# Layer 0's depthwise convolution: 24 scaled taps, summed by accumulating DMAs before and by additions on POOL after

## The chip, the core and the metric

The kernel runs on one core of one Trainium2 chip. The metric is the device time of one execution in microseconds (us). A core has five engines, each with an instruction queue of its own that is worked off in order: PE (TensorE, matmuls), DVE (VectorE), ACT (ScalarE), POOL (GpSimd) and SP (SyncE, which here only issues DMAs). On-chip data lies in SBUF as 128 partitions by some number of columns; matmul results lie in PSUM. Engines wait for one another through semaphores.

## The reference

The model is a two-layer diffusion backbone over 256 context tokens and 1024 latent tokens of width 1024. All arithmetic is float32. Layer 0 runs attention beside a convolution branch. This is the branch that the change touches, once for the context and once for the latent tokens:

```python
def conformer_conv(p, w, b, g, beta):
    a, gate = jnp.split(p, 2, axis=-1)                    # p: 1024 columns of h @ w_in
    u = depthwise_conv(a * jax.nn.sigmoid(gate), w, b)    # 31 taps, 512 channels
    return jax.nn.silu(layer_norm(u, g, beta))
...
y_lat = jnp.concatenate([attn_l, conv_l], axis=-1) @ w_out
```

The rest (attention, the gated feed-forward with a width-3 convolution, and layer 1 with a long convolution and a recurrence) is computed before and after alike.

## The kernel before

Activations lie channel by channel: 128 channels on the partitions, tokens along the columns. The 512 convolution channels are four groups c = 0 to 3 of 128. `l0_conv` forms the gated input `u` of a group (128 x 1295: 256 context columns, a gap of 15 zeros, 1024 latent columns); `conv_taps` sums its 31 shifted and scaled copies. The middle tap starts the sum `conv` on DVE (L709). Most others are one DVE instruction each (`stt`, L1192), which reads `u` and `conv` and writes `conv`. For groups 0, 1 and 2, eight of the 31 taps (`PTAPS`) go another way: ACT scales the shifted input into a buffer `ctap` (L722), and POOL's queue issues a DMA that adds this buffer to a second sum, `acc2`, in SBUF (L723). `acc2` has one buffer, cleared by POOL (L716), and is added to `conv` on DVE when the taps are done (L1188, called at the end of `conv_taps`). The profile and the listings of order call this tile `acc`. There are three `ctap` buffers, and they are also the buffers through which two sets of modulation weights (`adaw`) are loaded at that time.

Beside this work run the projections for attention. `l0_block` computes query, key and value for four head groups, 10 blocks of 128 tokens each, so 40 results `z` of 128 x 256. Each takes 24 matmuls on PE, squares with row sums and a copy on ACT (L779, L781), a scaling of the sums on DVE (`qkms`, L782), a reciprocal root of 128 x 4 numbers on POOL (`rs_r`, L427), the rotary products on DVE (`rt` and `z`, L1188), a multiplication of 128 x 256 on POOL (`z<-z,rs_r`, L1188), and a store to HBM. Weights come by `wunit`: a load by SP, a rounded copy on ACT (`whi`, L331), and the remainder on POOL (`wlo`, 128 x 1024, L332).

When the projections are done, `attention_all` begins. Before the first attention step, `stack_gen(0)` reads the first head group back, and POOL splits it into pieces `zst` (L981, L984, L986), which PE transposes (`zT`, L993). The normalisation of the convolution (`mu`, L849) follows among the first attention steps.

The order on each engine is not the order of the text: a scheduler arranges the instructions of this part when the program is built, and the engines then keep that order.

Of the kernel before, what the change touches and what calls it, by code (L numbers as in the profile page):

```python
# [13 lines left out]
ALU = mybir.AluOpType  # L14
# [233 lines left out]
class Kern:  # L248
# [457 lines left out]
    def conv_taps(self, c, u, acc, pool):  # L706
        nc = self.nc
        w = self.col("cw", 4, CW)
        nc.vector.tensor_scalar(out=acc, in0=u, scalar1=w[:, c, 15:16], scalar2=self.col("cb")[:, c:c + 1],  # L709
                                op0=ALU.mult, op1=ALU.add)  # L710
        taps = [j for j in range(CW) if j != 15]
        n = self.PTAPS[c]
        pt = taps[::len(taps) // n][:n] if n else []
        if n:
            acc2 = pool.tile([P, UL], F32, name="acc2", tag="acc2", bufs=1)
            nc.gpsimd.memset(acc2, 0.0)  # L716
        for j in pt + [j for j in taps if j not in pt]:
            s = j - 15
            a, b = max(0, -s), min(UL, UL - s)
            if j in pt:  # L720
                t = pool.tile([P, UL], F32, name="ctap", tag="ctap", bufs=3)
                nc.scalar.activation(t[:, a:b], u[:, a + s:b + s], AF.Copy, scale=w[:, c, j:j + 1])  # L722
                nc.gpsimd.dma_start(out=acc2[:, a:b], in_=t[:, a:b], accum_op=ALU.add)  # L723
            else:
                for o in range(a, b, self.VCUT):
                    e = min(b, o + self.VCUT)
                    self.stt(acc[:, o:e], u[:, o + s:e + s], w[:, c, j:j + 1], acc[:, o:e])
            yield 0.3 if j in pt else 1.45
        if n:
            self.add(acc, acc, acc2)  # L730
        if "conv" in self.dbg:
            nc.sync.dma_start(out=self.dbg["conv"][c], in_=acc)
# [1217 lines left out]
```

## Time and profile before

| | |
|---|---|
| time, 3 runs | median 3854.68 us (3852.33 to 3864.87) |
| profiled execution | 3860.75 us, of which 3858.7 us are the span from the first to the last instruction |
| mean granted TensorE clock | 0.962 |
| busy share of the span | PE 91%, DVE 59%, POOL 35%, ACT 32% |
| DMA issued through POOL's queue (software_dynamic) | 27648 packets, 35.76 MB |

How to read the rows. A row of a timeline gives the start and the duration in us, the engine, the line, the operation and its operands, and in brackets how long the engine had stood idle before it and what ended that. A row of groups gives a count, the busy time in us with the mean in ns, and the idle time in front with those that ended it. A row by tile or by line gives the shortest, median and longest duration in ns and the first and last start. A row of waits says who waited for whom: the total in us, how often, and the longest. A row of windows gives the busy time of each engine in one stretch of the span, then the granted clock, the busy share of the DMA engines and GB/s. All times in the text count from the start of the span.

### The profile page before, as it was taken

How to read it: one execution, taken by the hardware profiler on the slowest of the kernel's cores; microseconds unless marked ns; L12 is line 12 of the kernel's file. 1: busy time of each engine (PE TensorE's matmuls, PEld its weight loads, DVE VectorE, ACT ScalarE, POOL GpSimd, SP SyncE). 2: the span in 40 equal slices, each digit the busy share in tenths (PEclk: the TensorE clock that was granted, in tenths of full speed). 3: DMA queues.
4: the chain of work that ended last, by engine and by line, in shares of the span. 5: the costliest groups of instructions: out<-in, count | busy, mean ns of one | idle time of the engine just before them, and what ended most of it. 6: DMA issues, size and time to landing. Idle time of an engine off the chain costs nothing.

```text
span 3858.7 us, 47940 instructions
## 1 busy us (share of the span) xinstructions
PE 3516.5 (91%) x18708; PEld 2924.3 (76%) x18708; DVE 2289.8 (59%) x2847; ACT 1248.0 (32%) x2123; POOL 1334.2 (35%) x1003
## 2 busy tenths in 40 slices
PE   7988688888899999999999899999878899999998
PEld 4768466776687888888888778977666778888886
DVE  5977456666326666655555689455698554343435
ACT  4135566666333211122222422222112342222222
POOL 3248331100152111123333554355566642222223
PEclk9999789999999999999999899999898999999999
DMA  5376111000223223212222367433345311111111
GB/s 204 118 189 142 59 60 33 21 19 25 101 71 99 77 93 106 73 54 72 81 77 72 120 199 208 140 98 96 117 147 195 129 58 49 45 48 50 44 50 55
DMA packets 204017, 356.39 MB, mean 92 GB/s; under 512 B 23632, under 2 KB 124560, under 8 KB 203792
## 3 DMA queue, kind: packets, MB, share of 16 engines
q1 hardware_dynamic: 172240, 311.22, 24.8%
q0 software_dynamic: 27648, 35.76, 4.4%
q10 hardware_dynamic: 3904, 6.36, 0.5%
q8 instruction: 148, 2.42, 0.3%
q14 instruction: 77, 0.63, 0.1%
HBM read 275.04 MB, written 62.39 MB: 87 GB/s over the span
## 4 chain that ended last, share of the span: by engine, by line
PE 65%; DVE 12%; issue 4%; ACT 3%; DMA 3%; POOL 1%; SPq 0%; POOLq 0%; ACTq 0%; DVEq 0%
PE dl L338 13%; PE dl L339 13%; PE dl L340 13%; PE pj L338 2%; PE pT L1048 2%; PE pj L339 2%; PE pj L340 2%; DVE nm L1025 2%; PE o L1059 2%; DVE pl L1053 2%; PE S L1008 1%; PE dc L338 1%; PE dc L340 1%; PE dc L339 1%; PE S L1009 1%
## 5 line engine op out<-in xcount | busy, mean ns | idle before, releaser
L332 POOL TENSOR_TENSOR wlo<-wraw,whi 128x1024 fp32r<-128x1024 f32 (+1 forms) x226 | 567.4, 2516 | 1289.0 <-ACT whi L331 1288.8
L339 PE MATMUL dl<-hl,whi 128*128 128x512 f32 x1920 | 763.2, 398 | 3.8 <-POOL hl L1188 2.9
L338 PE MATMUL dl<-hh,whi 128*128 128x512 f32 x1536 | 607.0, 396 | 11.9 <-DVE fc L1099 8.7
L340 PE MATMUL dl<-hh,wlo 128*128 128x512 f32 x1536 | 607.9, 396 | 0.0
L331 ACT CAST whi<-wraw 128x1024 fp32r<-128x1024 f32 (+1 forms) x226 | 225.1, 1005 | 887.3 <-PE dl L339 415.2
L339 PEld LDWEIGHTS dl<-hl,whi 128*128 128x128 f32 x1920 | 362.9, 189 | 88.2 <-POOL hl L1188 4.6
L338 PEld LDWEIGHTS dl<-hh,whi 128*128 128x128 f32 x1536 | 289.3, 188 | 80.7 <-issue 7.0
L1097 DVE SCALAR_TENSOR_TENSOR fc<-dl,cols,fc 128x1023 f32<-128x1023 f32 x84 | 107.4, 1279 | 408.6 <-ACT fc L1096 408.6
L340 PEld LDWEIGHTS dl<-hh,wlo 128*128 128x128 f32 x1536 | 289.3, 188 | 68.7
L872 DVE SCALAR_TENSOR_TENSOR x<-dl,modT,x 128x1024 f32<-128x1024 f32 x160 | 204.1, 1277 | 113.7 <-PE dl L340 112.2
L338 PE MATMUL dl<-gs,whi 128*128 128x512 f32 x640 | 253.2, 396 | 9.1 <-DVE fc L1099 9.1
L339 PE MATMUL dl<-gs,whi 128*128 128x512 f32 x640 | 250.2, 391 | 0.0
L340 PE MATMUL dl<-gs,wlo 128*128 128x512 f32 x640 | 250.0, 391 | 0.0
L1053 DVE TENSOR_TENSOR pl<-pT,ph 128x512 fp32r<-128x512 f32 x252 | 167.5, 685 | 65.9 <-ACT ph L1052 65.3
L1048 PE MATMUL pT<-ident,p 128*128 128x128 f32 x1008 | 166.8, 288 | 41.6 <-DVE pl L1053 34.5
L1052 ACT CAST ph<-pT 128x512 fp32r<-128x512 f32 x252 | 142.7, 587 | 153.5 <-PE pT L1048 152.2
L1025 DVE TENSOR_REDUCE nm<-S 128x1 f32<-128x1280 f32 (+1 forms) x120 | 153.0, 1275 | 51.5 <-PE S L1009 47.1
L1059 PE MATMUL o<-ph,vs 128*128 128x256 f32 x504 | 147.0, 305 | 36.9 <-ACT ph L1052 18.9
L1048 PEld LDWEIGHTS pT<-ident,p 128*128 128x128 f32 x1008 | 121.5, 146 | 64.4 <-DVE pl L1053 48.4
L1192 DVE SCALAR_TENSOR_TENSOR conv<-u,cols,conv 128x1287 f32<-128x1287 f32 (+14 forms) x96 | 160.4, 1698 | 0.9
L338 PE MATMUL dl<-hl,whi 128*128 128x512 f32 x384 | 155.0, 405 | 1.7 <-ACT whi L331 0.8
L1059 PE MATMUL o<-pl,vs 128*128 128x256 f32 x504 | 152.3, 325 | 2.2 <-DVE pl L1053 2.2
(373 smaller groups left out, 8390.9 us busy)
## 6 DMA issues: line engine op xcount, KB each, us to landing
wraw<-in_wup SPq DMA_DIRECT2D x88, 512.0 KB, 3.5
adaw<-in_adaw SPq DMA_DIRECT2D x128, 256.0 KB, 2.8
wraw<-in_wdn SPq DMA_DIRECT2D x44, 512.0 KB, 3.5
adaw<-in_adaw SPq DMA_DIRECT2D x32, 512.0 KB, 4.1
df<-in_dftf POOLq DMA_DIRECT2D x64, 256.0 KB, 3.8
wraw<-in_w1f SPq DMA_DIRECT2D x24, 512.0 KB, 3.7
x<-in_xT SPq DMA_DIRECT2D x16, 640.0 KB, 10.1
spd<-so SPq DMA_DIRECT2D x68, 128.0 KB, 2.2
```

The lines of the kernel that those rows point to most:

```text
L331: nc.scalar.copy(hi[:, :cols], raw[:, :cols])
L332: nc.gpsimd.tensor_tensor(out=lo[:, :cols], in0=raw[:, :cols], in1=hi[:, :cols].bitcast(F32), op=ALU.subtract)
L338: mm(out, lhsT=lh, rhs=rh, start=first, stop=False)
L339: mm(out, lhsT=lh, rhs=rl, start=False, stop=False)
L340: mm(out, lhsT=ll, rhs=rh, start=False, stop=last)
L872: nc.vector.scalar_tensor_tensor(out=xl, in0=pl, scalar=self.mod(l, j, m, 0), in1=xl, op0=ALU.mult, op1=ALU.add)
L1025: nc.vector.tensor_reduce(out=nm[:, i:i + 1], in_=s, op=ALU.max, axis=AX.X, negate=True)
L1048: nc.tensor.transpose(pt[:, (2 * a + i) * P:(2 * a + i + 1) * P], p[:, kc * P:(kc + 1) * P], self.ident)
L1052: nc.scalar.copy(ph, pt)
L1053: nc.vector.tensor_tensor(out=pl, in0=pt, in1=ph.bitcast(F32), op=ALU.subtract)
L1059: nc.tensor.matmul(o, lhsT=vs[:, kc], rhs=x[:, a * 256:a * 256 + 256], start=(kc == 0 and j == 0), stop=(kc == nk // P - 1 and j == 1))
L1192: self.nc.vector.scalar_tensor_tensor(out=out, in0=a, scalar=s, in1=b, op0=ALU.mult, op1=op)
```

## The change

The DMA that adds a scaled tap to `acc2` becomes a POOL instruction that adds two SBUF tiles. The scaling on ACT, the taps on DVE, the buffers and the final addition stay as they are.

```diff
             if j in pt:
                 t = pool.tile([P, UL], F32, name="ctap", tag="ctap", bufs=3)
                 nc.scalar.activation(t[:, a:b], u[:, a + s:b + s], AF.Copy, scale=w[:, c, j:j + 1])
-                nc.gpsimd.dma_start(out=acc2[:, a:b], in_=t[:, a:b], accum_op=ALU.add)
+                self.add(acc2[:, a:b], acc2[:, a:b], t[:, a:b], pool=True)
```

`self.add(..., pool=True)` issues one `tensor_tensor` on POOL (L1188). There are 24 of them, each over 128 partitions and 1280 to 1294 columns.

The scheduler also arranges this part anew on all engines; from the first attention steps on, the order on PE, DVE, ACT and POOL is that of before. POOL's queue is shown at two places. The first is where group 1's taps begin (`acc_1098` is its `acc2`), among the reciprocal roots and products of the first head group. Before:

```order
L427 TENSOR_TENSOR rs_r<-qkms,mhalf 128x4 x2
L1188 TENSOR_TENSOR z<-z,rs_r 128x256 x2
L723 DMA acc_1098<-ctap 128x1280
L723 DMA acc_1098<-ctap 128x1283
L1188 TENSOR_TENSOR z<-z,rs_r 128x256
L427 TENSOR_TENSOR rs_r<-qkms,mhalf 128x4
L723 DMA acc_1098<-ctap 128x1286
L332 TENSOR_TENSOR wlo<-wraw,whi 128x1024
```

With the change:

```order
L427 TENSOR_TENSOR rs_r<-qkms,mhalf 128x4
L1188 TENSOR_TENSOR acc_1098<-acc_1098,ctap 128x1280
L1188 TENSOR_TENSOR acc_1098<-acc_1098,ctap 128x1283
L1188 TENSOR_TENSOR z<-z,rs_r 128x256
L427 TENSOR_TENSOR rs_r<-qkms,mhalf 128x4
L1188 TENSOR_TENSOR z<-z,rs_r 128x256
L1188 TENSOR_TENSOR acc_1098<-acc_1098,ctap 128x1286
L332 TENSOR_TENSOR wlo<-wraw,whi 128x1024
```

The additions take the places of the DMA issues, one reciprocal root and two products earlier than these stood.

The second place is the end of the projections in POOL's queue, where group 2's last taps (`acc_1609`) meet the first pieces `zst` for the attention. Before, the last of the eight DMAs stands ahead of nine more instructions of the projections, and the pieces follow without any tap between them:

```order
L723 DMA acc_1609<-ctap 128x1288
L1188 TENSOR_TENSOR z<-z,rs_r 128x256
L427 TENSOR_TENSOR rs_r<-qkms,mhalf 128x4
L1188 TENSOR_TENSOR z<-z,rs_r 128x256 x2
L427 TENSOR_TENSOR rs_r<-qkms,mhalf 128x4 x3
L1188 TENSOR_TENSOR z<-z,rs_r 128x256 x2
L981 CAST zst<-zl 128x3x64 x4
L986 TENSOR_TENSOR zst<-zl,zst 128x128 x2
```

With the change, three of the eight additions stand among the pieces:

```order
L981 CAST zst<-zl 128x3x64 x4
L986 TENSOR_TENSOR zst<-zl,zst 128x128
L1188 TENSOR_TENSOR acc_1609<-acc_1609,ctap 128x1294
L986 TENSOR_TENSOR zst<-zl,zst 128x128 x3
L1188 TENSOR_TENSOR z<-z,rs_r 128x256 x3
L974 CAST vs<-p 128x10x64
L984 TENSOR_TENSOR zst<-zl,zst 128x3x64 x4
L1188 TENSOR_TENSOR acc_1609<-acc_1609,ctap 128x1291
L975 TENSOR_TENSOR vs<-p,vs 128x10x64
L981 CAST zst<-zl 128x3x64 x2
L986 TENSOR_TENSOR zst<-zl,zst 128x128 x2
L1188 TENSOR_TENSOR acc_1609<-acc_1609,ctap 128x1288
```

They have moved behind the whole of the projections' reciprocal roots, into the stretch that PE's first transposes wait for.

## The prediction

> **What bounds the kernel now.** The page and the view of windows come first, because the change touches one stage only: the 24 DMAs on line 723 start between 183 and 380 us of a span of 3858.7 us, and behind the first attention steps every engine keeps its order. So what counts is by how much the start of the attention moves. What follows is one long dependent program with PE busy 91% of the span, and I let it move with that start, one for one.
>
> ```profile
> span 3858.7 us, 47940 instructions
> ...
> core 0: us, PE busy (x) PEld busy (x) DVE busy (x) ACT busy (x) POOL busy (x), PEclk, DMA share, GB/s
> 181.00:238.00 57.00, 51.11 (x298) 41.97 (x297) 31.38 (x23) 19.86 (x36) 17.64 (x12) 0.97 0.73 171
> 238.00:325.00 87.00, 76.59 (x513) 62.12 (x512) 72.95 (x129) 40.04 (x178) 62.59 (x46) 0.92 0.69 178
> 325.00:411.00 86.00, 63.91 (x477) 59.81 (x475) 44.30 (x127) 37.60 (x206) 69.23 (x90) 0.85 0.53 129
> ```
>
> The reader is to see POOL. Over the span it is busy 35%, but from 238 to 411 us it is busy 62.59 + 69.23 = 131.8 of 173 us, as much as anything but PE. It stands idle for 41.2 us there.
>
> Then the chain of waits and the timelines at the end of this stage:
>
> ```profile
> 407.65 0.41 POOL zst L986
> ...
> 409.02 1.66 POOL zst L984 x3
> ...
> 410.73 0.38 PE zT L993
> ```
>
> ```profile
> 384.57 0.28 PE L340 MATMUL qkl<-whi,hl 128*128 128x256 f32 x1
> 395.73 1.05 PE L993 MATMUL zT<-identr,zst 128*128 128x128 f32 x4 [10.88 <-POOL zst L984]
> ```
>
> PE has its last projection at 384.6 us, stands still for 10.88 us, and gets the first transposes when POOL delivers `zst`. The chain that ended last begins in POOL's queue too. These pieces stand behind nearly all other POOL work of the stage, so **the attention starts when POOL has worked off its queue.** Whatever lengthens that queue by more than its idle time delays the kernel.
>
> **What goes.** These waits belong to the accumulating DMAs. The first group is from 238 to 411 us on POOL, the second from 181 us on all engines:
>
> ```profile
> POOL rs_r L427 <- DVE qkms L782: 16.2, 7, 4.7
> POOL acc L723 <- DMA acc<-ctap: 9.4, 5, 3.1
> ...
> POOL acc L723 <- ACT adasb L371: 4.8, 1, 4.8
> POOL zst L981 <- PE zT L993: 3.5, 2, 3.0
> POOL acc L723 <- ACT ctap L722: 2.2, 1, 2.2
> POOL acc L723 <- DMA zd<-z: 1.6, 1, 1.6
> ```
>
> ```profile
> ACT ctap L722 <- DMA acc<-ctap: 44.3, 14, 6.1
> ...
> DVE qkms L782 <- ACT z L779: 26.3, 14, 5.9
> DVE conv L1188 <- DMA acc<-ctap: 20.5, 3, 14.3
> ...
> PE qkl L338 <- ACT z L781: 10.1, 5, 4.1
> ...
> PE adaps L365 <- DMA adaw<-in_adaw: 7.6, 3, 4.3
> ```
>
> ```profile
> DMA to landing us min/median/max: 5.1/5.5/9.5
> ```
>
> ```profile
> 236.88 1.51 DVE L1188 TENSOR_TENSOR conv<-conv,acc 128x1295 f32<-128x1295 f32 x1 [14.35 <-DMA acc<-ctap]
> ```
>
> Each of the 24 DMAs lands in 5.5 us (median) and the next must wait for it, so eight of them form a chain. POOL waits 9.4 + 4.8 + 2.2 + 1.6 = 18.0 us ahead of the 16 DMAs of groups 1 and 2. ACT waits 44.3 us for a free `ctap`; the rows of `z` stand behind it, DVE waits for these, and PE for its PSUM. DVE stands still for 14.35 us ahead of 236.88, until group 0's DMAs are done.
>
> **What comes.** The issue of a DMA takes POOL 0.92 us; an addition is longer. The nearest rows are POOL's additions a little later, when the DVE leaves it alone, and `wlo` and the other POOL work of this stage:
>
> ```profile
> L1188 POOL TENSOR_TENSOR acc<-acc,sq 128x512 f32<-128x512 f32 x4 | 5.1, 1274 | 54.6 <-ACT sq L435 54.5
> ...
> L1188 POOL TENSOR_TENSOR acc<-acc,sq 128x256 f32<-128x256 f32 x2 | 1.5, 728 | 0.1
> ```
>
> ```profile
> L723 POOL DMA_DIRECT2D acc<-ctap x24: 859/905/1081, 183.1 to 379.6; - x24
> ...
> L332 POOL TENSOR_TENSOR wlo<-wraw,whi x9: 2370/2685/4280, 190.9 to 353.0; 128x1024 fp32r<-128x1024 f32 x9
> ...
> L427 POOL TENSOR_TENSOR rs_r<-qkms,mhalf x40: 999/1308/2916, 240.0 to 389.4; 128x4 f32<-128x4 f32 x40
> ...
> L1188 POOL TENSOR_TENSOR z<-z,rs_r x40: 602/874/1878, 241.2 to 393.7; 128x256 f32<-128x256 f32 x40
> ```
>
> From 256 to 512 columns the time grows by 1274 - 728 = 546 ns, 2.13 ns a column. 1287 columns are 775 more than 512: 1.27 + 1.65 = **2.9 us** undisturbed. `wlo` agrees: 2.37 us at its shortest, plus 263 columns more, is 2.93 us.
>
> Undisturbed is not how POOL runs here. DVE and POOL hold one another up:
>
> ```profile
> 281.71 1.55 DVE L1192 SCALAR_TENSOR_TENSOR conv<-u,cols,conv 128x1290 f32<-128x1290 f32 x1
> ...
> 283.99 3.64 DVE L1192 SCALAR_TENSOR_TENSOR conv<-u,cols,conv 128x1289 f32<-128x1289 f32 x1
> ```
>
> ```profile
> 240.02 1.07 POOL L427 TENSOR_TENSOR rs_r<-qkms,mhalf 128x4 f32<-128x4 f32 x1 [0.39 <-DVE qkms L782]
> ...
> 282.40 3.87 POOL L332 TENSOR_TENSOR wlo<-wraw,whi 128x1024 fp32r<-128x1024 f32 x1
> ```
>
> ```profile
> L332 POOL TENSOR_TENSOR wlo<-wraw,whi 128x1024 fp32r<-128x1024 f32 x9 | 26.1, 2905 | 2.8 <-ACT whi L331 2.8
> ...
> L984 POOL TENSOR_TENSOR zst<-zl,zst 128x192 fp32r<-128x192 f32 x10 | 5.7, 599 | 0.0
> L986 POOL TENSOR_TENSOR zst<-zl,zst 128x128 fp32r<-128x128 f32 x10 | 4.4, 459 | 0.0
> ```
>
> `wlo` at 282.40 takes 3.87 in place of 2.37 us, since DVE works until about 284; then the tap at 283.99 takes 3.64 in place of 1.55 us, until `wlo` is out of the way. I take as the surcharge of an addition what `wlo` pays on average in this stage: nine in 26.1 us (2.90 each), less 2.37, is 0.5 us. So 3.4 us each. The bounds are 2.9 us, and 2.9 + (4.28 - 2.37) = 4.8 us, the surcharge of the longest `wlo`.
>
> **Group 0** (183 to 238 us) I cost at nothing. POOL is busy 17.64 of 57 us there; eight additions at 3.4 us less eight issues add 8 x 2.5 = 20 us, and there is room. Its DMA chain ends shortly before 236.88 us; the additions, with three `wlo` among them, need 8 x 3.4 + 3 x 2.9 = 36 us from 183 and end near 220 to 230. What is queued behind them is `wlo` of the next weights, with several us to spare. DVE gets its 14 us back and starts group 3's taps and the first `qkms` earlier, by up to 8 us on POOL (the first `rs_r` now starts at 240.02). If this cover is gone, the first head group's weights come late, by a few us.
>
> **Groups 1 and 2** are the term that counts, from 238 to 411 us. POOL's busy time of 131.8 us loses 16 x 0.92 = 14.7 and gains 16 x 3.4 = 54.4: 171.5 us. The idle time of 41.2 us loses the 18.0 above. Of the other 23.2, the waits for `qkms` (16.2) lie mostly before group 1's first tap, when PE has not yet delivered, and go on; additions fill a part. The waits for `zT` (3.5) stay. I keep 18 us. 171.5 + 18 = 189.5 against 173: **+17 us.** The earlier start (up to -8) and the delay that additions cause to `rt`, `z` and `qkms` on DVE (some 2 us for each that meets one, as the tap at 283.99 shows, thus new waits of `rs_r`) I set against one another. Three additions stand among the pieces `zst`; they are in the 16.
>
> Behind a waiting addition stand reciprocal roots and products of the projections: these hold the eight buffers of `z`, thus ACT and PE. That is the same queue, not a second term.
>
> **The sum.** The profiled execution took 3860.75 us; it would become 3877.8. It lies 6 us above the median of three runs, which I take as the base: 3854.7 + 17 = **3872 us.**
>
> The bounds: with 2.9 us each, all idle time but the 3.5 gone, and the earlier start kept whole: 131.8 - 14.7 + 46.4 + 3.5 - 8 = 159, thus -14 us. With 4.8 us each and the 23.2 us of idle kept: 131.8 - 14.7 + 76.8 + 23.2 = 217, thus +44 us.
>
> **Where a rule of the Trainium skill speaks.** The profile shows the mutual delay above, but also `rs_r` at 240.02, which took its usual 1.07 us beside a running tap. The Trainium skill, page "SBUF — State Buffer", states that DVE and GpSimd share a port pair that is "an exclusive lock, not a bandwidth split", for the whole instruction, and also against DVE instructions with two SBUF inputs. The tap and `wlo` agree; the undisturbed `rs_r` shows that not every POOL instruction holds it throughout. The rule taken at its word is the second rival.
>
> **Rivals.** *First: the additions fit into the idle time.* For it: the 41.2 us of idle, and the loss of ACT's 44.3 us of waits, behind which `qkms` and so `rs_r` had waited. The net addition is 54.4 - 14.7 = 39.7 us, which is just less than the idle. It decides if nearly all waits of `rs_r` for `qkms` go. Then the queue ends between -12 and +8 us, about 3853 us. Against it: POOL was all but full before in part of the stage, and the projections come at PE's pace.
>
> *Second: DVE and POOL as one resource.* From 238 to 391 us DVE's work with two SBUF inputs is these groups:
>
> ```profile
> L1192 DVE SCALAR_TENSOR_TENSOR conv<-u,cols,conv 128x1281 f32<-128x1281 f32 (+14 forms) x29 | 47.6, 1643 | 0.1
> L1188 DVE TENSOR_TENSOR z<-z,rgc 128x192 f32<-128x192 f32 x64 | 18.2, 323 | 0.0
> L1188 DVE TENSOR_TENSOR rt<-z,rgs 128x192 f32<-128x192 f32 x64 | 18.1, 325 | 0.3
> ...
> L1188 DVE TENSOR_TENSOR z<-z,rt 128x256 f32<-128x256 f32 x32 | 15.4, 492 | 0.2
> ```
>
> That is 99 us; with 1.55 for each tap some 96. POOL at its shortest: 40 `rs_r` of 1.0, 40 `z` of 0.6, five `wlo` of 2.37 (the other four of the nine lie ahead), 5.7 + 4.4 and the smaller ones for the pieces, say 14, and 16 additions of 2.9: 136 us. One after the other 232 against 173, less the 14 us that DVE gains at the start: +45 us, 3900 us. It decides if `rs_r` holds DVE up for its whole time. Against it stands the row at 240.02; without the 40 us of `rs_r` this sum gives +5.
>
> *Third, the other side: ACT's release is worth more than POOL's load.* If POOL keeps up as in the first rival and PE no longer stands for ACT's waits, PE works through the projections without its gaps. Those that end on ACT are 10.1 us, and those on the modulation weights, whose `ctap` buffers come free earlier, 7.6 us: about -18 us, 3837 us. It decides if POOL has the pieces ready less than 10 us behind PE's last projection. Against it: POOL must then do 40 us more work in 18 us less.
>
> **How the numbers follow.** The forecast, POOL's queue late by 8 to 28 us, gets 0.50; the first rival 0.25, the second (+28 and more) 0.17, the third 0.08. About 0.3%, 11.6 us, is what a measurement of this kernel can tell from no change. Slower than that are most of the forecast (0.43) and the second rival: 0.60. Within it are 0.07 of the forecast and 0.24 of the first rival: 0.31. Faster: 0.09. The range goes over the bounds, -14 to +45 us with the second rival's sum: 3841 to 3900. It leaves out the third rival and a part of the second, about 0.14.
>
> **What would show it.** In the profile after, the additions should take 2.9 us at the shortest and 3 to 4 on average. ACT should wait little for `ctap`. POOL should be busy over 90% from 250 us to the first transposes, and PE's first `zT` should stand at 405 to 425 in place of 395.7 us, behind a gap that ends on POOL. From there on all intervals should be as before. The forecast is wrong if PE's gap ahead of `zT` ends on something else, if the additions stretch beyond 5 us, or if a later stage changes its length.

## The result, and the profile after

| | before | after |
|---|---|---|
| time, median of 4 runs each | 3856.36 us (3852.33 to 3864.87) | 3880.64 us (3875.73 to 3883.32) |
| profiled execution | 3860.75 us | 3880.82 us |
| span | 3858.7 us | 3878.6 us |
| mean granted TensorE clock | 0.962 | 0.959 |
| DMA issued through POOL's queue | 35.76 MB | 19.93 MB |

The ratio is 1.0051 (95% interval 1.0033 to 1.0068): about 0.5% or 20 us slower, and 8.6 us above the predicted time.

The view of windows of the kernel after, over the stage and the 29 us behind it:

```profile
core 0: us, PE busy (x) PEld busy (x) DVE busy (x) ACT busy (x) POOL busy (x), PEclk, DMA share, GB/s
181.00:238.00 57.00, 53.09 (x294) 39.66 (x291) 48.34 (x24) 19.84 (x36) 44.70 (x13) 0.97 0.33 101
238.00:325.00 87.00, 72.41 (x496) 60.56 (x496) 82.67 (x116) 36.12 (x166) 68.33 (x37) 0.92 0.30 96
325.00:411.00 86.00, 62.30 (x468) 60.44 (x467) 64.99 (x138) 37.32 (x206) 86.00 (x78) 0.84 0.22 69
411.00:440.00 29.00, 14.94 (x61) 10.88 (x61) 5.24 (x6) 11.94 (x28) 20.33 (x35) 0.56 0.19 57
```

From 325 to 411 us POOL has no idle time at all: 86.00 of 86. In front of that it stands idle for 87 - 68.33 = 18.7 us. DVE has grown too: 82.67 + 64.99 us where the prediction's first view showed 72.95 + 44.30.

PE's timeline at the end of the projections, and the chain of waits there:

```profile
390.24 0.28 PE L340 MATMUL qkl<-whi,hl 128*128 128x256 f32 x1
408.41 1.05 PE L993 MATMUL zT<-identr,zst 128*128 128x128 f32 x4 [17.90 <-POOL zst L984]
...
419.25 1.05 PE L993 MATMUL zT<-identr,zst 128*128 128x128 f32 x4 [6.91 <-POOL zst L984]
```

```profile
424.77 0.41 POOL zst L986
...
426.15 1.66 POOL zst L984 x3
...
427.85 0.38 PE zT L993
...
431.07 3.37 PE mu L849 x8
```

The last piece `zst` comes at 427.81 in place of 410.68 us, and with it all that follows: +17.1 us. The first matmul `mu` behind it stands at 430.87, before at 413.74 (the chain's row at 431.07 had its counterpart at 413.94). On PE these 17 us have three parts. Its last projection ends 5.7 us later than before (390.5 against 384.8), its gap behind it is 17.90 in place of 10.88 us, and a second gap among the transposes is 6.91 in place of 2.36 us.

The groups of instructions on POOL and DVE from 181 to 425 us, first before, then after:

```profile
L427 POOL TENSOR_TENSOR rs_r<-qkms,mhalf 128x4 f32<-128x4 f32 x40 | 57.6, 1469 | 17.0 <-DVE qkms L782 16.2
L1188 POOL TENSOR_TENSOR z<-z,rs_r 128x256 f32<-128x256 f32 x40 | 35.3, 920 | 0.9 <-DVE z L1188 0.7
...
L723 POOL DMA_DIRECT2D acc<-ctap x24 | 22.0, 917 | 84.0 <-ACT z L774 42.9 <-DMA acc<-ctap 30.4 <-ACT adasb L371 4.8
```

```profile
L1188 POOL TENSOR_TENSOR acc<-acc,ctap 128x1280 f32<-128x1280 f32 (+7 forms) x24 | 82.5, 3438 | 39.9 <-ACT ctap L722 39.5
L427 POOL TENSOR_TENSOR rs_r<-qkms,mhalf 128x4 f32<-128x4 f32 x40 | 54.9, 1382 | 16.4 <-DVE qkms L782 16.2
L1188 POOL TENSOR_TENSOR z<-z,rs_r 128x256 f32<-128x256 f32 x40 | 34.1, 863 | 2.3 <-issue 1.8 <-DVE qkms L782 0.4
```

Issues of 22.0 us have become additions of 82.5 us; POOL's other work has kept its length, and its wait for `qkms` is 16.2 us in both. On DVE, in the same view:

```profile
L1192 DVE SCALAR_TENSOR_TENSOR conv<-u,cols,conv 128x1281 f32<-128x1281 f32 (+14 forms) x44 | 75.5, 1722 | 0.4
...
L1188 DVE TENSOR_TENSOR rt<-z,rgs 128x192 f32<-128x192 f32 x64 | 18.1, 325 | 0.3
```

```profile
L1192 DVE SCALAR_TENSOR_TENSOR conv<-u,cols,conv 128x1282 f32<-128x1282 f32 (+14 forms) x45 | 95.4, 2126 | 0.5
L1188 DVE TENSOR_TENSOR rt<-z,rgs 128x192 f32<-128x192 f32 x64 | 27.9, 476 | 0.6 <-ACT z L781 0.6
```

The first pair is before, the second after. Taps and rotary products on DVE, which the change does not touch, take 20 and 10 us more; some 2 us of the 20 are one tap more that falls into the window.

### The profile page after: what moved, and what is told of

Read it like the earlier page. It is cut to its first block, busy times and chain, and to the rows that moved or that the text cites. A ratio compares the mean times of both kernels' runs of the same rounds, so it can differ in the third digit from the quotient of the medians.

```text
span 3878.6 us, 47920 instructions
## 1 busy us (share of the span) xinstructions
PE 3520.8 (91%) x18708; PEld 2928.1 (75%) x18708; DVE 2330.9 (60%) x2847; ACT 1248.6 (32%) x2123; POOL 1405.5 (36%) x1003
## 3 DMA queue, kind: packets, MB, share of 16 engines
q0 software_dynamic: 24192, 19.93, 2.3%
## 4 chain that ended last, share of the span: by engine, by line
PE 68%; DVE 10%; issue 4%; ACT 3%; POOL 2%; DMA 1%; SPq 0%; POOLq 0%; ACTq 0%; DVEq 0%
PE dl L338 14%; PE dl L339 14%; PE dl L340 13%; PE pj L338 2%; PE pj L339 2%; PE pj L340 2%; PE pT L1048 2%; DVE nm L1025 2%; PE o L1059 2%; DVE pl L1053 2%; PE dc L338 1%; PE S L1008 1%; PE dc L340 1%; PE dc L339 1%; PE S L1009 1%
## 5 line engine op out<-in xcount | busy, mean ns | idle before, releaser
L332 POOL TENSOR_TENSOR wlo<-wraw,whi 128x1024 fp32r<-128x1024 f32 (+1 forms) x226 | 576.6, 2557 | 1291.2 <-ACT whi L331 1274.1
L1192 DVE SCALAR_TENSOR_TENSOR conv<-u,cols,conv 128x1287 f32<-128x1287 f32 (+14 forms) x96 | 178.8, 1892 | 1.0
```

Source lines behind the costliest of these rows:

```text
L332: nc.gpsimd.tensor_tensor(out=lo[:, :cols], in0=raw[:, :cols], in1=hi[:, :cols].bitcast(F32), op=ALU.subtract)
L1192: self.nc.vector.scalar_tensor_tensor(out=out, in0=a, scalar=s, in1=b, op0=ALU.mult, op1=op)
```

## The experiments

The question was which part of the change costs the 17 us, and whether POOL's own work or the mutual delay of DVE and POOL makes them. "Shift" is the first `mu` matmul against 413.7 us. The fastest kernel below ran twice, and its shift was -7.8 and -4.9 us, so a difference of 3 us between two shifts tells nothing. Each ratio is that to the kernel before on the same chip.

| kernel | ratio (95%) | last projection ends | gap before first zT | shift of mu |
|---|---|---|---|---|
| before | 1 | 384.8 | 10.88 | 0 |
| after | 1.0051 (1.0033 to 1.0068) | 390.5 | 17.90 | +17.1 |
| e1 POOL adds group 0 only | 0.9995 (0.9985 to 1.0004) | 383.9 | 12.97 | +1.1 |
| e2 POOL adds groups 1, 2 only | 1.004 (1.0025 to 1.0055) | 394.2 | 19.93 | +17.1 |
| e3 scaled taps not added | 0.9944 (0.9928 to 0.996) | 371.2 | 9.06 | -15.5 |
| e4 DVE adds all | 0.9995 (0.9976 to 1.0013) | 380.0 | 9.06 | -6.7 |
| e5 after, without group 3's taps | 0.9966 (0.9951 to 0.9982) | 368.5 | 20.87 | -7.7 |
| e6 all taps on DVE | 0.9993 (0.9981 to 1.0005) | 382.7 | 9.06 | -4.0 |
| e7 POOL adds group 0, rest DVE taps | 0.997 (0.9959 to 0.9982) | 378.9 | 9.06 | -7.8 |
| e8 POOL adds group 0, DVE adds 1, 2 | 1.0015 (1.0005 to 1.0024) | 389.4 | 9.06 | +2.7 |
| e9 before, without group 3's taps | 0.9968 (0.9953 to 0.9982) | 373.2 | 13.59 | -9.0 |
| e10 additions of groups 1, 2 twice | 1.0136 (1.0113 to 1.016) | 398.6 | 16.16 | +29.1 |
| e11 as e7 with ten taps | 0.9997 (0.9985 to 1.0009) | 384.3 | 9.06 | -2.4 |
| e12 e7 again | 0.9985 (0.9973 to 0.9996) | 381.8 | 9.06 | -4.9 |

The gap never gets shorter than 9.06 us. What it is longer has two sources. In the kernel after, e2, e5 and e10, POOL still has additions, roots and products in its queue when PE has done its projections. In the kernel before, e1 and e9 it has none left: DVE stands still until the last accumulating DMA has landed, `qkms` is behind that sum in DVE's queue, and POOL waits for `qkms`. DVE's and POOL's rows there, of the kernel before and then of e9:

```profile
385.39 1.51 DVE L1188 TENSOR_TENSOR conv<-conv,acc 128x1295 f32<-128x1295 f32 x1 [3.64 <-DMA acc<-ctap]
```

```profile
387.05 3.48 POOL L427 TENSOR_TENSOR rs_r<-qkms,mhalf 128x4 f32<-128x4 f32 x3 [3.72 <-DVE qkms L782]
```

```profile
376.40 1.51 DVE L1188 TENSOR_TENSOR conv<-conv,acc 128x1295 f32<-128x1295 f32 x1 [7.72 <-DMA acc<-ctap]
```

```profile
378.07 3.47 POOL L427 TENSOR_TENSOR rs_r<-qkms,mhalf 128x4 f32<-128x4 f32 x3 [4.70 <-DVE qkms L782]
```

So the kernel before does not start its attention late because of a full queue on POOL. There the last projections and, by 10.88 - 9.06 = 1.8 us, the last DMA set it.

### Which group costs it: e1 and e2

```diff
-                self.add(acc2[:, a:b], acc2[:, a:b], t[:, a:b], pool=True)
+                if c == 0:                                   # e2: c > 0
+                    self.add(acc2[:, a:b], acc2[:, a:b], t[:, a:b], pool=True)
+                else:
+                    nc.gpsimd.dma_start(out=acc2[:, a:b], in_=t[:, a:b], accum_op=ALU.add)
```

> POOL additions for group 0 alone; groups 1 and 2 keep the accumulating DMAs. Theory (POOL's queue from 238 us on sets the start of the attention; group 0 falls into a stretch where POOL has room): within 6 us of before, mu starts within 6 us of 413.7 us. Rival A (the additions delay DVE's taps in the early stretch, and this delay is carried on): a third or more of the loss, +7 us or more.

> POOL additions for groups 1 and 2; group 0 keeps the DMAs. Theory: nearly the whole loss of the change, +15 to +22 us, POOL busy without a gap from about 290 us to the attention, mu at 428 to 434 us. Rival A (loss from the early stretch): +12 us at most.

Measured: 3858.72 us against 3861.06 (e1) and 3876.05 us (e2). Group 0 alone shifts the attention by 1.1 us, groups 1 and 2 alone by 17.1, as much as the change. So group 0 costs nothing against its DMAs. In e2 only one addition stands among the pieces `zst`, in the change three, and the shift is the same: where the additions stand among the pieces is not the cause.

### The additions taken away, and given to DVE: e3 and e4

```diff
-                self.add(acc2[:, a:b], acc2[:, a:b], t[:, a:b], pool=True)
+                self.add(acc2[:, a:b], acc2[:, a:b], t[:, a:b])              # e4; e3 has no line here
```

> The eight scaled taps of groups 0, 1 and 2 are computed by ACT but not added to the sum at all, neither by DMA nor by POOL (left out of the result). Theory: POOL's queue loses 14.7 us of DMA issues and 18 us of waits against before, the attention starts earlier: -5 to -18 us against before. Rival B (PE's projections or DVE set the start of the attention, POOL only seems to): within 4 us of before, since PE's and DVE's work is that of before.

> The 24 additions are done by DVE in place of POOL, about 1.5 us each. Theory (POOL's own queue): POOL is relieved as in the run without additions, so the time is within 8 us of that run, and below before: -2 to -15 us. Rival C (DVE and POOL are one resource, and their sum sets the stage): the stage holds 16 x 1.5 = 24 us in place of 46 us of additions, so about half of the loss of the change stays, +5 to +12 us.

Measured: e3 (its output lacks the scaled taps) 3838.90 us and a shift of -15.5 us; e4 3857.89 us and -6.7. By its ratio e3 is 21.6 us faster than the kernel before, of which the start of the attention shows 15.5; its rival, no change, is out. Without additions and without DMAs the attention starts 32.6 us earlier than in the change, so the additions, not the missing DMAs or the scaling on ACT, are what delays it. On DVE the same 24 additions cost less than on POOL, but not nothing: e4 begins its attention 8.8 us behind e3, a little more than the theory allowed, and not behind the kernel before, as the rival wanted. Its time can't confirm the 6.7 us: the ratio gives -2 us, with an interval from -9 to +5.

### DVE's taps beside the additions: e5 and e9

```diff
-            else:
+            elif c < 3:                      # e5 from the change, e9 from the kernel before
```

> The changed kernel without the 30 outer taps of group 3 on DVE (left out of the result), which DVE does between about 223 and 335 us beside POOL's additions. Theory (POOL's own instructions, undisturbed, make up most of the queue): mu starts 6 to 14 us earlier than in the changed kernel's 431 us, so at 417 to 425 us, by what the mutual delay had cost POOL, and POOL stays busy over 90% from 325 us on. Rival C (DVE's and POOL's times add up to the stage): 30 taps of 1.5 us, 45 us, fall out of the sum, and mu starts at PE's limit, before 408 us.

> The kernel before (accumulating DMAs), with group 3's thirty outer taps left out on DVE, as the run before did with the change's POOL additions: there the first mu came at 406.0 (7.7 us ahead of the kernel before, 24.8 ahead of the change). This gives the fourth corner. If the additions' price is POOL's own queue, they cost about the same without group 3's taps: mu 20 to 27 us earlier than in the kernel before, 387 to 394, limited by PE, which cannot have its first transposes sooner than 9.1 us behind its last projection (the shortest gap of all runs). Rival: the additions cost something only because DVE's taps run beside them: then this kernel is no better than the one with additions, mu 5 to 11 us earlier, 403 to 409.

Group 3's taps run on DVE beside the additions of groups 1 and 2. Measured: 3849.83 us (e5) and 3846.03 us (e9). Against the kernel before the two ratios are the same. The additions shift `mu` by 17.1 us when group 3's taps run, and by 1.3 (-9.0 to -7.7) when they don't. **Here the theory fell twice**: e5 did not stay near the change, and e9 was not 20 us ahead of e5. Both starts lie where the rivals had them (406.0 and 404.7 us), though e5 not at PE's limit, since its gap is 20.87 us. POOL's rows from 181 to 425 us in e5, then in e9, whose additions are DMAs:

```profile
L1188 POOL TENSOR_TENSOR acc<-acc,ctap 128x1280 f32<-128x1280 f32 (+7 forms) x24 | 78.4, 3269 | 39.6 <-ACT ctap L722 39.3
L427 POOL TENSOR_TENSOR rs_r<-qkms,mhalf 128x4 f32<-128x4 f32 x40 | 45.4, 1142 | 13.3 <-DVE qkms L782 13.2
L1188 POOL TENSOR_TENSOR z<-z,rs_r 128x256 f32<-128x256 f32 x40 | 26.8, 681 | 3.4 <-ACT ctap L722 1.5 <-DVE z L1188 1.0 <-DMA adaw<-in_adaw 0.7
```

```profile
L427 POOL TENSOR_TENSOR rs_r<-qkms,mhalf 128x4 f32<-128x4 f32 x40 | 47.1, 1218 | 23.4 <-DVE qkms L782 23.0
L1188 POOL TENSOR_TENSOR z<-z,rs_r 128x256 f32<-128x256 f32 x40 | 28.2, 752 | 4.4 <-DVE z L1188 4.0 <-POOL wlo L332 0.4
```

Against the change, POOL does the same work in e5 in 4.1 + 9.5 + 7.3 = 21 us less, most of it in the short instructions. The windows from 238 us to the last piece `zst`, e5 and then e9:

```profile
238.00:402.99 164.99, 131.96 (x982) 117.74 (x980) 100.06 (x218) 77.80 (x384) 144.82 (x133) 0.89 0.29 90
```

```profile
238.00:401.68 163.68, 136.78 (x999) 119.15 (x997) 76.01 (x225) 77.39 (x384) 112.00 (x135) 0.92 0.64 163
```

POOL is busy 112.0 of 163.7 us in e9 and so idle for 51.7, where the kernel before was idle for 40.9 (131.8 of 172.7 us). The additions add 144.8 - 112.0 = 32.8 us, and these now fit: the idle time falls to 20.2 us and the end moves by 1.3. So what an addition costs here is not its own duration: it costs what exceeds POOL's idle time, and DVE's taps set how much there is of that. The 1.3 us are a little flattering, because e9 still waits for its last DMA: without that, an estimate from its gap (13.59 - 9.06) puts it 4.5 us earlier, and the additions would cost some 6 us there, still far less than 17. These two runs don't tell apart the room that DVE leaves to POOL from a direct collision of taps and additions; the additions of groups 1 and 2 themselves became only 4 us shorter (52.0 to 47.9).

### Twice the additions: e10

```diff
+                if c > 0:
+                    self.add(acc2[:, a:b], acc2[:, a:b], t[:, a:b], pool=True)
```

> The change, with each of the 16 additions of groups 1 and 2 made twice (these taps count double in the output). Theory: POOL has no idle time left from 287 us to the transposes, so each further addition shows in full: 16 x 2.9 to 3.5 = 46 to 56 us behind the change, mu 63 to 73 us behind the kernel before, and the time 1.016 to 1.020 of it. Rival: the queue's length is made by waits for DVE, and further additions partly lie in them: less than 35 us behind the change.

Measured: 3911.4 us, 30.8 us above the change (33 by the two ratios); the first `mu` comes 29.1 us behind the kernel before, not 63 to 73. The windows from 325 us on, and the row of the additions:

```profile
325.00:411.00 86.00, 55.84 (x431) 54.63 (x429) 60.33 (x135) 31.72 (x190) 85.89 (x70) 0.87 0.20 64
411.00:440.00 29.00, 9.15 (x40) 6.06 (x40) 0.00 (x0) 8.31 (x18) 28.91 (x35) 0.50 0.11 36
440.00:480.00 40.00, 17.66 (x60) 13.19 (x59) 8.71 (x10) 15.46 (x23) 38.81 (x25) 0.59 0.09 25
```

```profile
L1190 POOL TENSOR_TENSOR acc<-acc,ctap x40: 2872/2955/4252, 182.9 to 476.4; 128x1280 f32<-128x1280 f32 x5, 128x1283 f32<-128x1283 f32 x5, 128x1286 f32<-128x1286 f32 x5, 128x1289 f32<-128x1289 f32 x5
```

POOL stays nearly full until 480 us, and the additions, of 2.96 us in the median, run to 476.4. The direction is the theory's, the size the rival's: 16 more additions, 47 us of POOL's time, bring 31. POOL does them among the first attention steps too, where in the change it has little to do:

```profile
440.00:480.00 40.00, 28.34 (x135) 21.75 (x133) 18.01 (x29) 20.92 (x35) 3.95 (x4) 0.73 0.05 15
```

Here it is the view of windows of the change, with POOL busy 3.95 of 40 us. The first `mu` of e10 comes 12 us behind that of the change, the next 32 (29.1 - 17.1 and 50.6 - 18.6). That a third of them is hidden there is a reading of these windows, not tested alone.

### Other ways to split the taps: e6, e7, e8, e11, e12

```diff
-    PTAPS = (8, 8, 8, 0)
+    PTAPS = (0, 0, 0, 0)         # e6
+    PTAPS = (8, 0, 0, 0)         # e7 and e12, with the change's additions on POOL
+    PTAPS = (10, 0, 0, 0)        # e11, likewise
```

```diff
+                self.add(acc2[:, a:b], acc2[:, a:b], t[:, a:b], pool=c == 0)          # e8, PTAPS as before
```

> No group takes the way by ACT: all taps are taps of DVE, 24 more of 1.47 us, nothing of it on POOL or ACT. Theory: POOL's queue is that of the run without additions, and DVE has no waits for ACT's buffers as in the run with additions on DVE, so between those two: mu at 398 to 407 us, -2 to -18 us against before. Rival D (DVE is now the bound, since its rotary products stand behind the taps): mu later than 410 us, no gain.

> Group 0's eight taps by ACT and POOL additions, in the stretch where POOL has room; groups 1 and 2 are all taps of DVE. Theory: POOL's queue behind 238 us is that of the run without additions, DVE has 16 taps more: mu at 396 to 406 us, -5 to -20 us against before. Rival D (DVE is the bound): mu later than 410 us.

> ACT scales as in the changed kernel; group 0's additions on POOL, those of groups 1 and 2 on DVE. Theory: close to the run with all additions on DVE, mu at 400 to 409 us, -2 to -14 us against before. Rival A (group 0's additions on POOL delay DVE in the early stretch and with it all that follows): later than that run's 407 us by 5 us or more.

> POOL additions for group 0 alone, DVE taps for groups 1 and 2, as in the fastest kernel so far, with ten taps of group 0 in place of eight on ACT and POOL. POOL stood idle for 13.7 of 57 us from 181 to 238 us there. Theory: the two taps go into that idle time and take 2 x 1.5 to 2 us from DVE: mu 1 to 5 us earlier than with eight, 9 to 13 ahead of the kernel before. Rival: ten scalings and additions end behind DVE's taps of group 0, whose last sum then waits and holds DVE's queue: mu 2 to 8 us later than with eight.

> The fastest kernel so far again (POOL additions for group 0, DVE taps for groups 1 and 2), on the same chip as the kernel with ten: 0.996 to 0.998 of the kernel before if the first result holds, with mu 6 to 9 us earlier; 0.999 to 1.001 if that result was chance.

Measured: 3857.67 (e6), 3850.99 (e7), 3869.36 (e8) against 3862.96 us before; 3858.74 (e11) and 3851.51 (e12) against 3859.75 us before. In all five the gap is at its floor of 9.06 us: POOL keeps up, and the pace of the projections is left. With every tap on DVE (e6) the kernel is as fast as before, and `mu` at 409.7 us misses the theory's 398 to 407. e7 came within its theory, at the late end (405.9 us). With eight taps of group 0 on ACT and POOL it is the fastest kernel that computes everything, 0.15 to 0.3% ahead of the kernel before in two measurements whose intervals both leave out 1; the repeat, 0.9985, fell between the two outcomes that e12 was to decide between. In e8 the scaled taps of groups 1 and 2 are added on DVE at 1.49 us each, hardly less than the 1.55 us of the tap that e7 has in its place, and e8 is slower by 0.15%. Its `mu` comes 9.4 us behind e4's, so its theory fell and rival A held. In the text of the kernels the two differ in group 0's additions alone: on DVE (e4) the first `rs_r` starts at 229.04 us, on POOL (e8) at 239.87. Group 0 on POOL is thus free against its DMAs, but not against the same additions on DVE. Ten taps in place of eight lost the gain: POOL is busy 52.64 of 57 us from 181 to 238 us in e11, and `mu` comes 2.5 to 5.4 us later. That is the rival's side, though with the 3 us of the repeat its size stays open.

## Why the prediction was right, and where its steps were not

The time was right, and so was the place: POOL's queue reaches its last piece `zst` 17.1 us late, where the term for groups 1 and 2 gave +17. As forecast, POOL is busy for 93% of the time from 250 us to the first transposes (147.4 of 158.4 us), and these stand at 408.41. Point by point:

**What the attention waits for** was read as POOL's queue, in the kernel before already. There it was not: POOL stood idle for 3.72 us ahead of the last reciprocal roots, after PE's last projection. The change takes the start of the attention from one limit, PE's projections and the last DMA, to another, POOL's queue. The sum below gives the end of that queue all the same, since it counts the idle time that stays as well as the work.

**An addition** was to take 3.4 us in groups 1 and 2. The view of groups of the kernel after, from 238 to 430 us:

```profile
L1188 POOL TENSOR_TENSOR acc<-acc,ctap 128x1280 f32<-128x1280 f32 (+7 forms) x16 | 52.0, 3253 | 1.8 <-ACT ctap L722 1.7
```

3.25 us each, 52.0 in place of 54.4; the shortest of all took 2.902 us, as the line through the smaller additions gave.

**The sum on POOL**: 189.5 us from 238 us to the last piece were predicted, with 18 us of idle kept. It took 427.8 - 238 = 189.8 us. The view of windows cut at the last piece:

```profile
238.00:411.00 173.00, 134.71 (x962) 121.00 (x961) 147.67 (x253) 73.44 (x372) 154.33 (x114) 0.88 0.26 82
411.00:427.81 16.81, 6.92 (x30) 4.39 (x29) 2.43 (x1) 4.31 (x12) 13.84 (x21) 0.50 0.12 39
```

POOL is busy 154.33 + 13.84 = 168.2 us and idle 21.6, where 171.5 and 18 were predicted: two errors of over 3 us that cancel, so the closeness is in part luck. What this sum took as given, POOL's busy time of 131.8 us, is not POOL's own: e9 shows that it is 112.0 of 163.7 us up to the last piece when group 3's taps are gone. From there the same sum gives 112.0 - 14.7 + 54.4 + 18 = 169.7 us, +6, and e5 against e9 measured +1.3. So the sum holds to a few us as a sum over one stage with DVE's load as it is, and the theory that e5 and e9 were built on, a price that stays when that load goes, does not.

**Group 0** at nothing was right (e1: +1.1 us), but not by its working. It gave DVE 14 us back and the first `rs_r` up to 8 us earlier. DVE's timeline in that stage, and POOL's at 204 and 240 us:

```profile
194.36 31.78 DVE L1192 SCALAR_TENSOR_TENSOR conv<-u,cols,conv 128x1280 f32<-128x1280 f32 x8
```

```profile
204.47 8.44 POOL L1188 TENSOR_TENSOR acc<-acc,ctap 128x1292 f32<-128x1292 f32 x2
```

```profile
240.13 1.05 POOL L427 TENSOR_TENSOR rs_r<-qkms,mhalf 128x4 f32<-128x4 f32 x1 [4.03 <-DVE qkms L782]
```

Eight taps take 31.78 us, 3.97 each in place of 1.55, beside additions of 4.2 us. DVE's busy time from 181 to 238 us grows by 48.34 - 31.38 = 17 us, more than the 14 us of idle that it lost. The first `rs_r` starts at 240.13, before at 240.02. **This step failed**: the early start did not come, and the 14 us are found again as stretched taps. That the stretching alone held it up is not shown: in e3, whose taps are not stretched, DVE waits 8.77 us for PE ahead of 231.28, and the first `rs_r` starts at 238.80 all the same; in e4 it starts at 229.04. The scheduler orders each of these kernels anew, and how much of it is the order stays open.

**The delay on DVE** was set against that early start and so cost nothing in the sum. It did cost: `rt` takes 476 in place of 325 ns. The last projection ends 5.7 us later; that this comes from DVE and not from POOL's fuller queue is not shown. On the queue's end it shows only in those 3.6 us of idle more.

**ACT** was to wait little for `ctap`. The view of waits from 181 to 430 us:

```profile
ACT ctap L722 <- POOL acc L1188: 34.3, 10, 8.4
...
DVE conv L1188 <- POOL acc L1188: 18.9, 1, 18.9
POOL rs_r L427 <- DVE qkms L782: 16.2, 5, 6.3
```

ACT waits 34.3 us, before 44.3: now for a queue in place of a chain of DMAs. The 20.5 us for which DVE waited ahead of its sums are 18.9 us, in one piece. These waits were not removed but turned to POOL.

**The later stages** were to keep their length. The shift of 17.1 us at `mu` is 19.9 us in the span, and the median is 24.3 us up. In the kernel that was measured twice the span differs from the shift by -1.3 and +3.8 us, so the 2.8 us up to the span are no more than that. The granted clock is 0.959 in place of 0.962. Among the runs of the kernel before on one chip, those at 0.959 took 3861 to 3869 us and those at 0.964 or more 3852 to 3858. That the change lowers the clock is not shown.

**The rivals.** The first (the additions fit) had 51.7 us of idle on POOL in e9, and 40.9 were not enough: it holds in e9's surroundings, not in the kernel's. The second (one resource) holds almost to the letter in group 0: the five additions and three `wlo` beside the eight taps from 194 to 226 us would take 5 x 2.9 + 3 x 2.37 + 8 x 1.55 = 34 us one after the other, and took 31.8. The Trainium skill, page "SBUF — State Buffer", section "SBUF: two separate sides", has a DVE instruction with two SBUF inputs and a GpSimd instruction that reads SBUF block one another for the whole instruction; these rows agree to within 2 us in 34. Over the stage the second rival gave too much, +45 against +17. It also reads e5 too high: thirty taps of 1.55 us are 46 us, and the attention came 24.8 us earlier. The third (ACT's release) did not come, since ACT was not released; without the additions, in e3, the projections do end 13.6 us earlier and `mu` comes 15.5 us earlier, near its -18.

## What to carry to other kernels

Where an engine's queue ends a stage, the sum over that stage (its busy time, plus the new work, plus the idle time that cannot be used) predicts the shift better than the cost of the new work alone, but it holds only with the other engines' load as it was. An engine whose queue ends the stage after a change need not have ended it before: here POOL's idle time just ahead of the pieces showed it. In these runs moving the additions from DMAs to POOL was free where POOL's idle time held them, with the stretching by DVE's work beside it (group 0, e1), and delayed what waits for POOL by the rest where it didn't (groups 1 and 2). Idle time that the change gave back to DVE beside POOL reappeared as longer DVE instructions.

## What the runs showed of the hardware that was not expected

DVE and POOL, both with long float32 instructions on SBUF, ran almost one after the other here: 8 taps of 1.55 us beside 8 POOL instructions took 31.8 of the 34 us of the plain sum, each side stretched (taps to 3.97 us, additions to 4.2). For POOL's short instructions the price is larger in proportion: a product `z` of 128 x 256 averages 863 ns in the change and 681 ns without group 3's taps beside it.
